# Setting a chunk's weights with a predicated copy, and moving half of the diagonal into the skip factor

## The chip, the cores and the metric

The kernel runs on one core of one Trainium2 chip. The metric is the time of one execution in microseconds (us) of device time. Five engines work side by side, each through its own queue in order: TensorE (PE, with its weight loads shown as PEld), VectorE (DVE), ScalarE (ACT), GpSimd (POOL) and SyncE (SP), which issues most DMAs.

## What is computed

Two layers of a bidirectional encoder trunk on a sequence of 2048 tokens with 1024 channels. The change lies in the second layer, in the Mamba-2 heads (8 heads of 64 channels in 2 groups, state size 128). Cut to what matters:

```python
def dir_inputs(dt_raw, d):
    dt = softplus(dt_raw + dt_bias[d])
    return xs * dt[..., None], dt * (-exp(a_log[d]))

x_fw, a_fw = dir_inputs(dt_f, 0)
x_bw, a_bw = dir_inputs(dt_b, 1)
y = (ssd_chunked(x_fw, a_fw, bm, cm)
     + rev(ssd_chunked(rev(x_bw), rev(a_bw), rev(bm), rev(cm)))
     + d_skip[:, None] * xs)
y = rms_norm(y.reshape(bsz, seq, WIDTH_D) * silu(dz), ssm_norm_g)
return concat([yc, y], -1) @ w_out        # then the residual and a layer norm
```

Inside a chunk, `ssd_chunked` multiplies three things for a query token i and a key token j: the product of C at i and B at j, the decay between the two tokens, and the input at j, which carries the factor dt of that direction. The forward direction holds for j up to and including i, the backward direction for j from i on. On the diagonal, j = i, both directions count and the decay is one.

## The kernel before, in words

The sequence is cut into 16 chunks of 128 tokens. The first layer and the input projections of the second run first; the last stage of the program, from about 2315 us on, is a loop over the chunks c = 0 to 15 that ends each chunk's Mamba-2 output, and behind it the output projection of the whole layer.

For a chunk, `Ssd.local` loads tokens (`tk`), B and C (`bc`), the gate (`dzl`) and the backward state (`sbl`). On PE it makes `pcb`, the products of B and C of both groups, 128 x 256 in one bank of PSUM. For each group g of four heads it makes the decay exponents in the bank `pd`: POOL (L1246) and ACT (L1249) fill `rr`, four matmuls sum it (L1250, L1251), and ACT writes the exponential into `E` (L1253). The weights `w`, 128 x 512 for a group, take dt of the forward direction where j <= i and dt of the backward one where j >= i: per head, ACT multiplies the triangle `le` by the forward dt (L1256), and DVE multiplies the triangle `ge` by the backward dt and adds (L1257). Then DVE multiplies `E` by `pcb` (L1259) and `w` by `E` (L1260).

`Ssd.forward` uses the weights one chunk later: the matmuls `py` (L1273), the skip term (POOL, L1276: tokens times `dskip`, a factor per head), the sum (L1277), the contributions of the two states (`pin` on PE L1281, `ti` on DVE L1285, added on POOL L1286), the state's update (`pu` L1211, `sf` L1219 and L1220), the gate (L1292), the norm (L1294 to L1297), a transpose into the bank `pt` (L1300) and `syo` (DVE, L1302). `OutProj.steps` is the output projection with the layer norm: it splits `syo` and the other heads' `yr` into a high and a low part (ACT L1003, DVE L1004), runs 48 matmuls a chunk into `oo` (L1032), and DVE, ACT and POOL do the rest (L1039 to L1050).

Three things tie the engines here. `E` has one buffer, the tag `cvt`. The bank `pd` is single too. `pcb` and `pt` share one bank, so the `pcb` of chunk c+1 can be made only when `syo` of the chunk before has read `pt`. The order on each engine is set by a scheduler at build time; the four queues are then fixed. In three of the chunks a pass over the other kind of heads (`pass_b`, with `pob`, `stw`, `opl`) is put between, up to about 2547 us.

Of the kernel before, what the change touches and what calls it, by code (L numbers as in the profile page):

```python
# [10 lines left out]
F32 = mybir.dt.float32  # L11
F32R = mybir.dt.float32r
I32 = mybir.dt.int32
AF = mybir.ActivationFunctionType
ALU = mybir.AluOpType
AX = mybir.AxisListType
# [3 lines left out]
P = 128  # L20
# [410 lines left out]
class Rec:  # L431
# [14 lines left out]
    def bank(self, name):  # L446
        return self.ps.tile([P, 512], F32, name=name, tag="rg", bufs=self.e.rg_bufs)
# [616 lines left out]
class Ssd:  # L1064
# [157 lines left out]
    def local(self, c, pool, bank):  # L1222

        e, nc = self.e, self.e.nc
        cs = slice(c * P, (c + 1) * P)
        k = self.cur[c] = Env()
        kp = self.kp
        k.tk = kp.tile([P, 768], F32, name="tk", tag="tk", bufs=2)
        nc.sync.dma_start(k.tk, self.tok[cs, :])
        k.bc = kp.tile([P, 4, P], F32, name="bc", tag="cvx", bufs=2)  # L1230
        nc.sync.dma_start(k.bc, self.xc[:, :, cs])
        k.dz = kp.tile([P, 512], F32, name="dzl", tag="sb", bufs=2)
        nc.sync.dma_start(k.dz, self.dz[cs, :])
        k.sb = kp.tile([P, 512], F32, name="sbl", tag="cva", bufs=2)
        nc.sync.dma_start(k.sb, self.sbd[c])
        pcb = bank("pcb")
        for g in range(2):
            nc.tensor.matmul(pcb[:, g * P:(g + 1) * P], k.bc[:, g], k.bc[:, 2 + g], start=True, stop=True)
        k.w = pool.tile([P, 2, 4, P], F32, name="w", tag="Q", bufs=2)
        for g in range(2):  # L1240
            pd = bank("pd")
            w = k.w[:, g]
            for d, (m1, m2) in enumerate((("gt", "le"), ("lt", "ge"))):
                r = pool.tile([P, 2, 4, P], F32R, name="rr", tag=f"T{d}", bufs=1)
                h0 = d * 8 + g * 4
                nc.gpsimd.tensor_tensor(r[:, 0], e.tri[m2].unsqueeze(1).broadcast_to([P, 4, P]),  # L1246
                                        self.aH[:, c, h0:h0 + 4].unsqueeze(2).broadcast_to([P, 4, P]), ALU.mult)
                for h in range(4):
                    nc.scalar.activation(r[:, 1, h], e.tri[m2], AF.Copy, scale=self.aL[:, c, h0 + h:h0 + h + 1])  # L1249
                nc.tensor.matmul(pd, e.trir[m1], r[:, 0], start=d == 0, stop=False)  # L1250
                nc.tensor.matmul(pd, e.trir[m1], r[:, 1], start=False, stop=d == 1)  # L1251
            E = kp.tile([P, 4, P], F32, name="E", tag="cvt", bufs=1)
            nc.scalar.activation(E, pd.rearrange("p (h i) -> p h i", h=4), AF.Exp)  # L1253
            for h in range(4):
                hh = g * 4 + h
                nc.scalar.activation(w[:, h], e.tri["le"], AF.Copy, scale=self.dt[:, c, hh:hh + 1])  # L1256
                nc.vector.scalar_tensor_tensor(w[:, h], e.tri["ge"], self.dt[:, c, 8 + hh:9 + hh], w[:, h],  # L1257
                                               ALU.mult, ALU.add)
            nc.vector.tensor_tensor(E, E, pcb[:, g * P:(g + 1) * P].unsqueeze(1).broadcast_to([P, 4, P]), ALU.mult)  # L1259
            nc.vector.tensor_tensor(w, w, E, ALU.mult)  # L1260

    def forward(self, c, pool, bank):
        e, nc = self.e, self.e.nc
        cs = slice(c * P, (c + 1) * P)
        h8 = lambda t: t.rearrange("p (h q) -> p h q", h=8)
        k = self.cur.pop(c)
        tk, bc, dz, sb = k.tk, k.bc, k.dz, k.sb
        if c == 0:
            self.sf = pool.tile([P, 512], F32, name="sf", tag="qm0", bufs=1)
            nc.gpsimd.memset(self.sf, 0.0)  # L1270
        py = bank("py")
        for hh in range(8):
            nc.tensor.matmul(py[:, hh * 64:(hh + 1) * 64], k.w[:, hh // 4, hh % 4], tk[:, hh * 64:(hh + 1) * 64],  # L1273
                             start=True, stop=True)
        acc = pool.tile([P, 512], F32, name="yacc", tag=f"{'kq'[c % 2]}m1", bufs=1)
        nc.gpsimd.tensor_tensor(h8(acc), h8(tk[:, :512]), self.dskip.unsqueeze(2).broadcast_to([P, 8, 64]), ALU.mult)  # L1276
        nc.vector.tensor_tensor(acc, py, acc, ALU.add)  # L1277
        for d, st in ((0, self.sf), (1, sb)):
            po = bank("pin")
            for g in range(2):  # L1280
                nc.tensor.matmul(po[:, g * 256:(g + 1) * 256], bc[:, 2 + g], st[:, g * 256:(g + 1) * 256],  # L1281
                                 start=True, stop=True)
            t = pool.tile([P, 512], F32, name="ti", tag=f"Sf{d}", bufs=1)
            eq = self.ed["qf" if d == 0 else "qb"][:, c, :].unsqueeze(2).broadcast_to([P, 8, 64])
            nc.vector.tensor_tensor(h8(t), h8(po), eq, ALU.mult)  # L1285
            nc.gpsimd.tensor_tensor(acc, acc, t, ALU.add)  # L1286
        if c < NC - 1:
            pu = self.update(self.weighted(c, 0, tk, pool), tk[:, 512:], bank)
            new = pool.tile([P, 512], F32, name="sf", tag=f"{'kq'[c % 2]}m0", bufs=1)
            self.step(new, self.sf, c, 0, pu)  # L1290
            self.sf = new
        nc.vector.tensor_tensor(acc, acc, dz, ALU.mult)  # L1292
        ss = pool.tile([P, 1], F32, name="sss", tag="ss", bufs=4)
        nc.scalar.activation(t, acc, AF.Square, accum_out=ss)  # L1294
        nc.gpsimd.tensor_scalar(ss, ss, 1.0 / 512, 1e-6, ALU.mult, ALU.add)
        nc.gpsimd.tensor_tensor(ss, ss, e.mhalf[:, 0:1], ALU.pow)
        nc.scalar.activation(acc, acc, AF.Copy, scale=ss)  # L1297
        pt = bank("pt")
        for i in range(4):
            nc.tensor.transpose(pt[:, i * P:(i + 1) * P], acc[:, i * P:(i + 1) * P], e.ident)  # L1300
        yo = pool.tile([P, 4, P], F32, name="syo", tag="kd", bufs=1)
        nc.vector.tensor_tensor(yo, pt.rearrange("p (a b) -> p a b", a=4),  # L1302
                                self.gcol.unsqueeze(2).broadcast_to([P, 4, P]), ALU.mult)
        return yo
# [50 lines left out]
def trunk(ctx, tc, i, out):  # L1355
    nc = tc.nc
    e = Env()
# [5 lines left out]
    def const(name, shape, dt=F32):  # L1363
        t = cp.tile(list(shape), dt, name=f"c_{name}")
        nc.sync.dma_start(t, i[name])
        return t
# [9 lines left out]
    def opened(name, side, **kw):  # L1376
        cm = tc.tile_pool(name=name, bufs=1, reuse_waits="tile", side=side, **kw)
        pools[name] = cm
        return cm.__enter__()
# [169 lines left out]
    hg = const("hgrn_g", [P, 1])  # L1549
    sg_ = const("ssm_g", [P, 4])  # L1550
    e.tri = {m: const(f"t_{m}", [P, P]) for m in TRI}
    e.trir = {}
    for m in ("gt", "lt"):
        e.trir[m] = cp.tile([P, P], F32R, name=f"r_{m}")
# [24 lines left out]
    kp = opened("conv", "left")  # L1579
# [104 lines left out]
def layout(inp):  # L1684

    f = lambda n: np.ascontiguousarray(inp[n])
    r = {}
# [28 lines left out]
    t, j = a[:, None], a[None, :]  # L1716
    for nm, m in (("gt", t > j), ("lt", t < j), ("le", t <= j), ("ge", t >= j)):
        r["t_" + nm] = m.astype(np.float32)
    lm = np.zeros((P, 5, 32), np.int32)
    i32 = np.arange(32)  # L1720
    for l in range(5):
# [21 lines left out]
```

## Time and profile before

| | us |
|---|---|
| median of 3 runs | 2748.59 |
| lowest and highest | 2747.47 to 2750.7 |
| the profiled execution, its own time | 2755.94 |
| its span from the first instruction to the last | 2754.1 |
| the last stage, from 2315 us on | 439 |

The profiled execution is one run with the profiler on; its rows show when each instruction started on its engine and how long it took. Over the whole span PE is busy 92%, DVE 54%, ACT 41% and POOL 48%; in the last stage DVE is busy six to nine tenths of each slice but the final one. An instruction's shown duration overlaps with the next one's by 0.06 to 0.09 us on DVE, so that an instruction shown with 0.68 us holds the queue for about 0.60.

### The profile page before, as it was taken

To read this page: it belongs to the slowest core of one execution; us is meant where nothing else is said; L and a number is where in the kernel's file an instruction comes from. 1 tells how busy PE (TensorE), PEld (TensorE's weight loads), DVE (VectorE), ACT (ScalarE), POOL (GpSimd) and SP (SyncE) were. 2 spreads that over 40 slices of the span, in tenths; PEclk is the share of its full clock that TensorE was granted. 3 is DMA by queue.
4 is the path that set the end of the run, shared out by engine and by line. 5 is a ranking of instruction groups with operands and counts; after the bars stand their busy time and mean duration, and the time that the engine had idled before them with its cause. 6 is when DMAs were issued, how large, how long until landed. Compare 5 with 4: busy or idle time off the path is not lost. (4 is left out here: it accounts for less than half of the span.)

```text
span 2754.1 us, 53110 instructions
## 1 busy us (share of the span) xinstructions
PE 2526.8 (92%) x20888; PEld 2125.2 (77%) x20888; DVE 1493.4 (54%) x2493; ACT 1122.9 (41%) x2355; POOL 1326.1 (48%) x1305
## 2 busy tenths in 40 slices
PE   7999999999999799998999999999999888788987
PEld 5877778887778677877788777888877677566776
DVE  6223335124433676765626356432625788687895
ACT  3152323244343644543323444232424453554652
POOL 4252325244442544434535556335534677575874
PEclk9999999999999899999999999999999999798998
DMA  8525434323365878775553335434436567543331
GB/s 275 159 99 169 145 115 132 115 95 106 109 221 181 253 210 234 202 205 167 173 201 126 106 124 177 136 127 131 134 105 207 169 200 235 182 148 112 117 115 62
DMA packets 269800, 432.46 MB, mean 157 GB/s; under 512 B 25936, under 2 KB 143600, under 8 KB 269552
## 3 DMA queue, kind: packets, MB, share of 16 engines
q1 hardware_dynamic: 267248, 420.69, 48.7%
q0 software_dynamic: 2304, 8.39, 0.8%
q8 instruction: 165, 2.70, 0.4%
q14 instruction: 83, 0.68, 0.1%
HBM read 296.60 MB, written 132.38 MB: 156 GB/s over the span
## 5 line engine op out<-in xcount | busy, mean ns | idle before, releaser
L186 POOL TENSOR_TENSOR wl<-wraw,wh 128x1024 fp32r<-128x1024 f32 (+2 forms) x116 | 290.5, 2524 | 293.9 <-ACT wh L185 293.0
L1032 PE MATMUL oo<-wo,yH 128*128 128x512 f32 x1024 | 309.9, 418 | 21.8 <-ACT yH L1003 20.2
L536 POOL TENSOR_TENSOR Kp<-Kp,T 128x256 f32<-128x256 f32 x144 | 125.7, 873 | 275.1 <-ACT F L492 111.7
L1032 PEld LDWEIGHTS oo<-wo,yH 128*128 128x128 f32 x1024 | 199.8, 201 | 65.3 <-ACT yH L1003 23.5
L860 POOL TENSOR_TENSOR nap<-nap,nasm 128x384 f32<-128x384 f32 (+2 forms) x128 | 115.7, 914 | 209.5 <-DVE nasm L859 192.2
L534 DVE TENSOR_TENSOR Kp<-Kp,T 128x256 f32<-128x256 f32 x144 | 103.7, 720 | 146.6 <-PE fine L459 60.2
L185 ACT CAST wh<-wraw 128x1024 fp32r<-128x1024 f32 (+2 forms) x116 | 116.8, 1052 | 154.5 <-PE obqk L205 27.4
L1032 PE MATMUL oo<-wo,yL 128*128 128x512 f32 x512 | 172.4, 405 | 3.0 <-DVE yL L1004 3.0
L532 DVE TENSOR_TENSOR Q<-Q,T 128x512 f32<-128x512 f32 x144 | 146.9, 1020 | 0.0
L885 PE MATMUL nay<-napts,nav 128*128 128x128 f32 (+1 forms) x832 | 121.5, 289 | 20.2 <-ACT napts L872 13.7
L885 PEld LDWEIGHTS nay<-napts,nav 128*128 128x128 f32 (+1 forms) x832 | 114.5, 202 | 31.3 <-ACT napts L872 16.1
L1154 DVE SCALAR_TENSOR_TENSOR cva<-cvx,cw,cva 128x512 f32<-128x512 f32 x96 | 104.2, 1098 | 30.5 <-ACT cva L1152 29.4
L1032 PEld LDWEIGHTS oo<-wo,yL 128*128 128x128 f32 x512 | 97.5, 193 | 23.5 <-DVE yL L1004 4.2
L205 PE MATMUL oqf<-hH,wh 128*128 128x512 f32 x256 | 104.8, 409 | 4.5 <-ACT wh L185 4.5
L205 PE MATMUL ox<-hH,wh 128*128 128x512 f32 x256 | 106.2, 415 | 0.0
L497 DVE COPY_PREDICATED S<-lmask,fine 128x128 f32<-128x128 int32 x160 | 43.7, 297 | 111.3 <-PE fine L459 111.2
L205 PE MATMUL ox<-hH,wl 128*128 128x512 f32 x256 | 102.7, 401 | 0.0
L205 PE MATMUL ox<-hL,wh 128*128 128x512 f32 x256 | 102.5, 400 | 0.0
L205 PE MATMUL oqf<-hL,wh 128*128 128x512 f32 x256 | 102.4, 400 | 0.0
L205 PE MATMUL oqf<-hH,wl 128*128 128x512 f32 x256 | 101.9, 399 | 0.5 <-POOL wl L186 0.5
L858 ACT ACTIVATE nap<-nap,namx 128x384 f32<-128x384 f32 (+2 forms) x128 | 79.2, 619 | 50.6 <-DVE namx L857 50.3
L156 POOL TENSOR_TENSOR hL<-hf,hH 128x512 fp32r<-128x512 f32 x36 | 50.2, 1403 | 96.9 <-ACT hH L155 96.9
(375 smaller groups left out, 7723.8 us busy)
## 6 DMA issues: line engine op xcount, KB each, us to landing
wraw<-in_o_w_dram SPq DMA_DIRECT2D x56, 512.0 KB
wraw<-in_e_w_dram SPq DMA_DIRECT2D x44, 512.0 KB
adw<-in_ada_w_dram SPq DMA_DIRECT2D x32, 512.0 KB
tk<-xtok SPq DMA_DIRECT2D x31, 384.0 KB
nat<-in_na_tab_dram SPq DMA_DIRECT2D x16, 640.0 KB
xt<-in_x_dram SPq DMA_DIRECT2D x16, 512.0 KB
adw<-in_ada_p_dram SPq DMA_DIRECT2D x16, 512.0 KB
naq<-aq SPq DMA_DIRECT2D x64, 128.0 KB
```

Of the source, the lines that this page charges most:

```text
L156: (nc.vector if d % 2 and not act else nc.gpsimd).tensor_sub(hL[:, d, :], hf, hH[:, d, :].bitcast(F32))
L185: nc.scalar.copy(h[:, sl], raw)
L186: (nc.vector if e.wl_dve else nc.gpsimd).tensor_sub(l[:, sl], raw, h[:, sl].bitcast(F32))
L205: nc.tensor.matmul(oo, a, b, start=d == 0 and m == 0, stop=d == ND - 1 and m == 2)
L532: nc.vector.tensor_tensor(qv, qv, view(tcur, toff + 1, [[nb - 1, 2], [2, n2], [0, s]]), ALU.mult)
L534: nc.vector.tensor_tensor(kv, kv, view(tcur, toff + nb + 1, [[2, n2], [0, s]]), ALU.mult)
L536: nc.gpsimd.tensor_tensor(kv, kv, view(tcur, toff, [[2, n2], [0, s]]), ALU.mult)
L858: nc.scalar.activation(p[:, :nk], p[:, :nk], AF.Exp, bias=mx, scale=-1.0, accum_out=sm)
L860: nc.gpsimd.tensor_tensor(p[:, :nk], p[:, :nk], sm.broadcast_to([P, nk]), ALU.mult)
L885: nc.tensor.matmul(s.yp[:, n, :], b.vs[:kb, n, j, :], s.pts[n][:kb, j, :], start=j == 0, stop=j == nj - 1)
L1032: nc.tensor.matmul(os[n], ops[m][0][:, c, :], ops[m][1][c][:, ns], start=x == 0, stop=x == 23)
L1154: nc.vector.scalar_tensor_tensor(acc, xr[:, k:k + SW], cw[:, i, k:k + 1], acc, ALU.mult, ALU.add)
```

## The change

The weights of a group are set by two instructions instead of eight. ACT writes the backward dt, spread over the columns, into all 512 columns (`nc.scalar.copy`), and DVE overwrites the places where j <= i with the forward dt by a predicated copy under an integer mask, `lei`, which is a new constant of 128 x 128 that SP loads once. The diagonal then holds the forward dt alone. Its backward share, dt of the backward direction times the product of B and C at the token itself, is added to the skip factor instead: DVE takes the diagonal of `pcb` (multiply by the identity into `own`, then a sum along the row into `cd`), multiplies it by the backward dt and adds `dskip`; the result `skip` is the factor in POOL's skip term. `own` lies in the same single buffer `cvt` as `E`.

```diff
         pcb = bank("pcb")
...
+        own = kp.tile([P, 2, P], F32, name="own", tag="cvt", bufs=1)
+        nc.vector.tensor_tensor(own, pcb[:, :2 * P].rearrange("p (g i) -> p g i", g=2),
+                                e.ident.unsqueeze(1).broadcast_to([P, 2, P]), ALU.mult)
+        cd = pool.tile([P, 2], F32, name="cd", tag="cd", bufs=2)
+        nc.vector.tensor_reduce(cd, own, AX.X, ALU.add)
+        k.skip = pool.tile([P, 2, 4], F32, name="skip", tag="skip", bufs=2)
+        nc.vector.tensor_tensor(k.skip, self.dt[:, c, 8:].rearrange("p (g h) -> p g h", g=2),
+                                cd.unsqueeze(2).broadcast_to([P, 2, 4]), ALU.mult)
+        nc.vector.tensor_tensor(k.skip, k.skip, self.dskip.rearrange("p (g h) -> p g h", g=2), ALU.add)
...
-            for h in range(4):
-                hh = g * 4 + h
-                nc.scalar.activation(w[:, h], e.tri["le"], AF.Copy, scale=self.dt[:, c, hh:hh + 1])
-                nc.vector.scalar_tensor_tensor(w[:, h], e.tri["ge"], self.dt[:, c, 8 + hh:9 + hh], w[:, h],
-                                               ALU.mult, ALU.add)
+            dts = [self.dt[:, c, d * 8 + g * 4:d * 8 + g * 4 + 4].unsqueeze(2).broadcast_to([P, 4, P]) for d in range(2)]
+            nc.scalar.copy(w, dts[1])
+            nc.vector.copy_predicated(w, e.lei.unsqueeze(1).broadcast_to([P, 4, P]), dts[0])
...
-        nc.gpsimd.tensor_tensor(h8(acc), h8(tk[:, :512]), self.dskip.unsqueeze(2).broadcast_to([P, 8, 64]), ALU.mult)
+        nc.gpsimd.tensor_tensor(h8(acc), h8(tk[:, :512]), k.skip.rearrange("p g h -> p (g h)").unsqueeze(2).broadcast_to([P, 8, 64]), ALU.mult)
...
+    e.lei = const("t_lei", [P, P], I32)
```

The scheduler orders the queues anew from about 2315 us on; what stands ahead of that is as before, save for the mask's load. On DVE, one chunk in the middle of the loop stood like this before (`syo` and `yL` belong to the chunk that is ending, `w` and `E` to the chunk that is prepared):

```order
L1302 TENSOR_TENSOR syo<-pt,c_ssm_g 128x512
L1277 TENSOR_TENSOR yacc<-py,yacc 128x512
L1285 TENSOR_TENSOR ti<-pin,edqf 128x512
L1285 TENSOR_TENSOR ti<-pin,edqb 128x512
L1004 TENSOR_TENSOR yL<-syo,yH 128x512
L1257 SCALAR_TENSOR_TENSOR w<-c_t_ge,dt,w 128x128
L1259 TENSOR_TENSOR E<-E,pcb 128x512
L1257 SCALAR_TENSOR_TENSOR w<-c_t_ge,dt,w 128x128 x4
L1220 TENSOR_TENSOR sf<-sf,pu 128x512
L1257 SCALAR_TENSOR_TENSOR w<-c_t_ge,dt,w 128x128 x2
L1260 TENSOR_TENSOR w<-w,E 128x512
L1257 SCALAR_TENSOR_TENSOR w<-c_t_ge,dt,w 128x128
```

On DVE after the change, the same place of a chunk near the end of the loop (`own` and `cd` are the diagonal, L1266 is the predicated copy):

```order
L1285 TENSOR_TENSOR yacc<-py,yacc 128x512
L1004 TENSOR_TENSOR yL<-syo,yH 128x512
L1266 COPY_PREDICATED w<-c_t_lei,dt 128x512
L1241 TENSOR_TENSOR own<-pcb,c_ident 128x256
L1266 COPY_PREDICATED w<-c_t_lei,dt 128x512
L1293 TENSOR_TENSOR ti<-pin,edqf 128x512
L1244 TENSOR_REDUCE cd<-own 128x2
L1300 TENSOR_TENSOR yacc<-yacc,dzl 128x512
L1246 TENSOR_TENSOR skip<-dt,cd 128x8
L1039 SCALAR_TENSOR_TENSOR r<-r,oo 128x512
L1248 TENSOR_TENSOR skip<-skip,dskip 128x8
```

What moved: the eight multiply-adds went, the two predicated copies stand in their place, and the first reader of `pcb` is now `own`, at once behind the first copy, where it had been the multiply of `E`.

On PE, around a transpose `pt` and the next `pcb`, after the change (L1260 and L1261 are now the `pd` matmuls, L1281 `py`, L1289 `pin`):

```order
L1260 MATMUL pd<-rr,r_gt 128x512
L1261 MATMUL pd<-rr,r_gt 128x512
L1308 MATMUL pt<-c_ident,yacc 128x128 x4
L1260 MATMUL pd<-rr,r_lt 128x512
L1261 MATMUL pd<-rr,r_lt 128x512
L1281 MATMUL py<-tk,w 128x64 x4
L1289 MATMUL pin<-sf,bc 128x256 x2
L1289 MATMUL pin<-sbl,bc 128x256 x2
L1238 MATMUL pcb<-bc 128x128 x2
L1032 MATMUL oo<-wo_23903,yH 128x512
```

And before, in one of the chunks where the same pieces stood together:

```order
L1250 MATMUL pd<-rr,r_lt 128x512
L1300 MATMUL pt<-c_ident,yacc 128x128 x4
L1251 MATMUL pd<-rr,r_lt 128x512
L1273 MATMUL py<-tk,w 128x64 x4
L1281 MATMUL pin<-sf,bc 128x256 x2
L1281 MATMUL pin<-sbl,bc 128x256 x2
L1238 MATMUL pcb<-bc 128x128 x2
L1250 MATMUL pd<-rr,r_gt 128x512
L1251 MATMUL pd<-rr,r_gt 128x512
L1211 MATMUL pu<-xw,tk 128x256 x2
```

What moved: behind `pcb` now stand the projection's matmuls, where the next `pd` had followed; `pcb` still stands behind `py` and both `pin`.

## Rows read from the trace of the kernel before

**Rows 1.** Busy time by stretch; the first line names the columns.
```profile
core 0: us, PE busy (x) PEld busy (x) DVE busy (x) ACT busy (x) POOL busy (x), PEclk, DMA share, GB/s
...
2402.00:2547.00 145.00, 121.78 (x568) 100.24 (x567) 115.42 (x168) 67.43 (x190) 92.09 (x93) 0.91 0.40 129
2547.00:2700.00 153.00, 138.74 (x672) 114.51 (x671) 137.74 (x196) 88.83 (x255) 112.19 (x113) 0.96 0.36 115
2700.00:2754.00 54.00, 41.48 (x183) 33.22 (x181) 26.88 (x42) 11.82 (x20) 20.81 (x22) 0.90 0.13 49
```

**Rows 2.** The chain that ended last, shares by line, 2547 to 2700 us.
```profile
by line: PE oo L1032 28.5%; DVE w L1257 25.3%; issue 4.7%; DVE r L1048 3.6%; PE pin L1281 3.6%; PE py L1273 3.4%; DVE w L1260 3.1%; DVE yL L1004 2.7%; DVE yacc L1292 2.5%; ACT rr L1249 2.2%; DVE E L1259 2.1%; DVE ti L1285 1.7%; DVE sf L1220
```

**Rows 3.** DVE's groups, 2402 to 2700 us: busy, mean ns | idle before, releasers.
```profile
L1257 DVE SCALAR_TENSOR_TENSOR w<-c_t_ge,dt,w 128x128 f32<-128x128 f32 x96 | 75.3, 835 | 2.3 <-ACT w L1256 2.3
...
L1260 DVE TENSOR_TENSOR w<-w,E 128x512 f32<-128x512 f32 x26 | 24.7, 951 | 0.3
...
L1259 DVE TENSOR_TENSOR E<-E,pcb 128x512 f32<-128x512 f32 x26 | 17.6, 677 | 7.5 <-ACT E L1253 3.8 <-PE pcb L1238 3.6
```

**Rows 4.** DVE in order of time in one chunk: start, us, instruction.
```profile
2616.93 0.67 DVE L1259 TENSOR_TENSOR E<-E,pcb 128x512 f32<-128x512 f32 x1
2617.53 4.17 DVE L1257 SCALAR_TENSOR_TENSOR w<-c_t_ge,dt,w 128x128 f32<-128x128 f32 x4
```

**Rows 5.** POOL in the same microseconds.
```profile
2618.12 1.09 POOL L1246 TENSOR_TENSOR rr<-c_t_le,aH 128x512 fp32r<-128x512 f32 x1
2619.17 1.33 POOL L1286 TENSOR_TENSOR yacc<-yacc,ti 128x512 f32<-128x512 f32 x1
2620.47 1.09 POOL L1203 TENSOR_TENSOR xw<-tk,edkf 128x512 f32<-128x512 f32 x1
```

**Rows 6.** Single lines over the whole span: ns min/median/max, first and last start, forms.
```profile
L1257 DVE SCALAR_TENSOR_TENSOR w<-c_t_ge,dt,w x128: 292/527/1446, 2318.8 to 2687.2; 128x128 f32<-128x128 f32 x128
L1260 DVE TENSOR_TENSOR w<-w,E x32: 672/692/1777, 2354.0 to 2713.8; 128x512 f32<-128x512 f32 x32
L497 DVE COPY_PREDICATED S<-lmask,fine x160: 274/297/309, 168.1 to 2323.8; 128x128 f32<-128x128 int32 x160
L396 DVE TENSOR_TENSOR st<-st,odz x32: 401/410/422, 1764.9 to 2334.6; 128x256 f32<-128x256 f32 x32
L1042 DVE BATCH_NORM_AGGREGATE mv<-bst x32: 180/200/210, 1004.6 to 2746.5; 128x2 f32<-128x12 f32 x32
L1256 ACT ACTIVATE w<-c_t_le,dt x128: 384/388/403, 2317.8 to 2679.0; 128x128 f32<-128x128 f32 x128
L1003 ACT CAST yH<-syo x16: 602/618/622, 2402.7 to 2734.1; 128x512 fp32r<-128x512 f32 x16
```

**Rows 7.** The chain's PE pieces, 2600 to 2650 us: start, us, what.
```profile
2610.64 0.24 PE pd L1250
...
2611.35 0.44 PE pt L1300 x4
...
2612.02 0.84 PE py L1273 x8
2612.85 1.80 PE pin L1281 x8
...
2635.81 0.44 PE pcb L1238 x4
2636.25 5.49 PE oo L1032 x24
...
2642.14 0.92 PE pu L1211 x4
```

**Rows 8.** Waits, 2402 to 2700 us: us in total, times, longest.
```profile
ACT E L1253 <- DVE w L1260: 17.4, 7, 6.9
...
PE pcb L1238 <- DVE syo L1302: 5.7, 3, 4.1
...
PE pd L1250 <- ACT E L1253: 4.3, 1, 4.3
```

More of the change, by code (lines that the diff above doesn't have):

```diff
@@ L1718, in layout @@
         r["t_" + nm] = m.astype(np.float32)
+    r["t_lei"] = (t <= j).astype(np.int32)
     lm = np.zeros((P, 5, 32), np.int32)
```

## The prediction, made before the changed kernel ran

> **What bounds the kernel now.** Read the busy time by stretch first, then the chain that ended last, then DVE's groups, and last two engines side by side. The change touches only the loop over chunks, so the stretches from 2402 us on are the ones to read; 12 of the 16 chunks have their weights made between 2402 and 2700 us (96 multiply-adds, 8 a chunk [rows 3]). In that stretch DVE is busy 115.4 of 145 us and then 137.7 of 153 us [rows 1]: 253 of 298. PE looks as busy, but its ends are modelled. What it needs is read from the chain's pieces [rows 7]: a chunk has two runs of 24 `oo` (2 x 5.49), 8 `pd` of 0.24, `pt` 0.44, 16 `py` (2 x 0.84), `pin` 1.80, `pcb` 0.44 and `pu` 0.92, together 18.2 us, against the 298 / 12 = 24.8 us that a chunk takes in the stretch as a whole. So PE has room, and DVE has little.
>
> The chain says the same. In 2547 to 2700 us the multiply-adds of L1257 hold 25.3% of it, second only to the projection [rows 2]: 0.253 x 153 = 38.7 us, 5.5 us for each of the 7 chunks there.
>
> Why they are so dear: one takes 292 ns at best, but 835 ns in the mean of the stretch [rows 3, 6]. Four of them in a row took 4.17 us [rows 4], one for each POOL instruction that ran in the same microseconds, each of 1.1 to 1.3 us [rows 5]. Which instructions suffer can be told apart. `E` times `pcb`, with one input in PSUM, takes 677 ns in the mean; `w` times `E`, of the same size with both inputs in SBUF, takes 951 [rows 3]. The predicated copy that the kernel has elsewhere, with its data in PSUM, never took over 309 ns in 160 times [rows 6]. So an instruction of DVE with two inputs in SBUF waits until POOL's present one is over, and eight small ones wait eight times.
>
> **The change part by part.** *Removed on DVE:* 96 multiply-adds, 75.3 us of DVE's time in the stretch [rows 3], 6.3 us a chunk.
>
> *Added on DVE, predicated copies:* 24, of 512 columns. The trace has this operation only with 128 columns and data in PSUM, 297 ns [rows 6]. Here mask and data both lie in SBUF. The lower bound is the instruction of that size that never waits, 677 ns, the upper one the longest that `w` times `E` took, 1777 ns [rows 3, 6]. I take the mean of `w` times `E`, by its kind of inputs the nearest row: 24.7 / 26 = 0.95, so 24 x 0.95 = 22.8 us.
>
> *Added on DVE, the diagonal:* `own` is 256 columns with one input in PSUM, as the row of L396: 410 ns [rows 6], less about 0.07 of overlap 0.34. The sum along the row reads 256 columns from one tile; no such operation is in the trace, and I take the same 0.34, between 0.20 (the aggregate on 12 numbers) and 0.68 (512 columns) [rows 3, 6]. Both: 12 x 0.68 = 8.2 us.
>
> *Added on DVE, the skip factor:* two instructions of 8 columns with two inputs in SBUF. Without a wait they cost what the aggregate costs, 0.20 less 0.07; with the full wait of the worst multiply-add (1446 - 292 ns) [rows 6] 1.15 us more. I add the mean wait of `w` times `E`, 951 - 677 = 0.27, and round to 0.35 with what the short overlap loses: 24 x 0.35 = 8.4 us, between 3 and 31.
>
> DVE's sum: 75.3 - 22.8 - 8.2 - 8.4 = 35.9 us less in the stretch, 3.0 a chunk. With the low ends it is 75.3 - 16.2 - 6.5 - 3 = 50; with the high ends 75.3 - 42.6 - 12.2 - 31 = -10, a loss.
>
> *How much of this shows.* In 2547 to 2700 us most of the removed time is on the chain (38.7 us, where 7 of 12 chunks hold 43.9 of the 75.3 us of multiply-adds), so the net share of it, 35.9 / 75.3 = 0.48, is gained: 38.7 x 0.48 = 18.5 us. From 2402 to 2547 us no chain is to be had; DVE stands idle 30 of 145 us there, and PE too waits more [rows 1]. The other 31.4 us of multiply-adds lie there, net 15; I count half, 7 us, since only some of DVE's queue can be what PE waits for in a stretch where both wait. Before 2402 and after 2700 us nothing is counted: in the tail no weights are made any more, and the first stretch waits for the last projections. Sum: 25.5 us.
>
> *ACT:* per chunk eight of 388 ns go and two writes of 512 columns come, 618 ns by the cast of that size [rows 6]: 1.9 us less. ACT is busy 88.8 of 153 us [rows 1] and holds little of the chain [rows 2], so this counts as nothing; what hides it is DVE's queue, and if that got so short that ACT was next, it would be a gain of at most 1.9 us a chunk. *POOL:* the same number of instructions; its skip term now waits for `skip`, which is made a chunk earlier, so nothing. *PE:* no instruction added. *SP:* one load of 64 KB with the other constants, over a millisecond ahead of its first use.
>
> *New waits.* `own` stands in DVE's queue behind one predicated copy, before `ti`, the gate and the layer norm's instructions, and needs `pcb`. On PE `pcb` stands behind `pt`, two `pd`, half of the `py`, and `pin`, which end 0.48 + 0.84 + 1.80 + 0.44 = 3.6 us after `pt`. In that time DVE does `syo`, `yacc` and `yL` at about 0.6 each and a copy at 0.95, 2.8 us, and `yL` waits for ACT's cast of 0.62 in between [rows 6]. The wait left is some 0.2 us, near the noise of the sum. Second, `E` can be filled only when the sum along the row has read `own`. So far it waited for `w` times `E` of the group before, 17.4 us in 7 times [rows 8]. The sum stands three to five instructions ahead of the reader of `E`, which covers ACT's exponential (about the 0.62 of the cast) or most of it. I cost both at nothing, and put the case that they aren't under the rivals.
>
> **A rule of the skill against the row.** The rows above show that 512 columns with both inputs in SBUF cost 951 ns and with one in PSUM 677. The Trainium skill, SBUF — State Buffer, section Who interferes with whom, says that a Vector instruction with two SBUF inputs contends with a GpSimd instruction that reads SBUF, that whichever starts first holds the shared port for its whole length, and that a reduction along the row does not contend. By that rule the predicated copies stay exposed to POOL and the result is as above; if a predicated copy did not contend, 24 x 0.27 = 6.5 us more of DVE's time would go and the gain would be about 30 us. No row shows a predicated copy with two SBUF inputs.
>
> **The rivals.** *1. More: PE sets the pace.* If DVE's relief counts whole in both stretches, the 298 us fall by all of the 36 us, and by 50 with the low ends. For it speaks the 18.2 us that PE needs in 24.8; against it, the shares of the chain in which DVE, PE and ACT alternate. Time, with the middle of the two, 43: 2748.6 - 43 = 2706.
>
> *2. Absorbed.* PE, POOL and ACT wait for each other as well: POOL is busy 112.2 of 153 us [rows 1], and its instructions have the other side of every wait with DVE. If the chain goes over to POOL and PE as soon as DVE is shorter, or the new order loses in its first chunks what the later ones gain, the gain is 0 to 5 us. Against it speaks that 25% of the chain is one line. Time: 2746.
>
> *3. Slower: `own` blocks DVE's queue.* If `pcb` is late, `own` holds everything behind it, the layer norm of the chunk included, and the sum behind it delays `E`, the `pd` of the second group and so PE. The price is the wait per chunk; it decides from 3.0 us on, where it eats all that DVE saves. Waits of such lengths occur: `pcb` waited up to 4.1 us for `syo`, `pd` 4.3 for `E` [rows 8]. With 4.1 in each of 12 chunks it is 12 x (4.1 - 3.0) = 13 us slower, 2762. Against it: `pcb` was late in 3 of the chunks alone.
>
> **How the numbers follow.** The profiled execution took 2755.9 us, 7.3 more than the median of the runs, 2748.6; I take the same 25.5 us from both: 2730.4 with the profiler, 2723 without. Chances: the forecast (10 to 38 us less) 0.64; rival 1 0.08; rival 2 0.17; rival 3 with the high ends of the new instructions 0.11. About 0.2% (5.5 us) is what a measurement of this kernel can tell from no change. Rival 2 lies within that line and counts as the same, with 0.01 of the case with the high ends: faster 0.64 + 0.08 = 0.72, same 0.18, slower 0.10. The range runs from 2703, which takes in most of rival 1, to 2747, about the middle of rival 2; some 0.15 is left out above and 0.04 below.
>
> **What would show it.** Right: L1257 is gone, the copies of L1266 take 0.9 to 1.0 us in the mean with a least value near 0.68, `own` near 0.41 always; DVE is busy about 215 us in the 12 chunks' stretch, which is 20 to 30 us shorter; the tail from the last `w` times `E` on is as long as before, 40 us (2713.8 to 2754 [rows 6]); the waits `own` <- `pcb` and `E` <- sum are a few us in all. Wrong: copies at 1.5 us or more, the two small instructions over 0.8 us each, a wait for `pcb` or for ACT's `E` of several us in each chunk, or a chain in which POOL has taken DVE's share.

## The result and the profile after

| | before | after |
|---|---|---|
| median, us | 2749.64 | 2715.24 |
| ratio after to before, 95% interval | | 0.9872, 0.9845 to 0.9898 |
| the same two kernels again, in other runs, us | 2751.30 | 2720.31 |
| ratio of these, 95% interval | | 0.9879, 0.9863 to 0.9895 |
| the profiled execution's span, us | 2754.1 | 2709.5 |

The kernel became 1.2 to 1.3% faster by the two ratios, 31 to 34 us by the medians, against 25.5 us in the forecast of 2723. The stretch ahead of the loop has the same instructions in all kernels here, save for the mask's load, but ends between 2300 and 2319 us from one profiled execution to another; why, no run here shows. Totals of single executions so differ by up to 19 us before the loop begins. The comparisons below therefore use the **loop time** of a profiled execution as well: from the last start of `cva`, an instruction of the first layer, to the end of the span. The rows of that mark, the kernel before and the one after (ns min/median/max, first and last start):

```profile
L1154 DVE SCALAR_TENSOR_TENSOR cva<-cvx,cw,cva x96: 735/752/2897, 1609.7 to 2312.3; 128x512 f32<-128x512 f32 x96
```
```profile
L1154 DVE SCALAR_TENSOR_TENSOR cva<-cvx,cw,cva x96: 736/752/2899, 1602.3 to 2304.3; 128x512 f32<-128x512 f32 x96
```

The loop takes 2754.1 - 2312.3 = 441.8 us before and 2709.5 - 2304.3 = 405.2 after, 36.6 less. A second profiled execution of the changed kernel gave 407.0. Cut at the same events (the layer norm's `mv` of chunks 0, 5 and 13), the loop has four pieces; the rows are cut to whole microseconds. Before:

```profile
core 0: us, PE busy (x) PEld busy (x) DVE busy (x) ACT busy (x) POOL busy (x), PEclk, DMA share, GB/s
2312.00:2412.00 100.00, 76.07 (x513) 63.95 (x512) 69.61 (x125) 51.97 (x159) 54.63 (x58) 0.80 0.58 197
2412.00:2547.00 135.00, 112.13 (x518) 92.25 (x518) 106.45 (x155) 64.50 (x184) 88.00 (x89) 0.90 0.40 130
2547.00:2714.00 167.00, 152.74 (x741) 126.29 (x740) 145.49 (x209) 92.00 (x260) 117.26 (x118) 0.96 0.35 112
2714.00:2754.00 40.00, 27.48 (x114) 21.43 (x112) 19.13 (x29) 8.64 (x15) 15.74 (x17) 0.87 0.10 40
```

After:

```profile
2304.00:2399.00 95.00, 73.57 (x515) 61.62 (x515) 66.35 (x112) 46.28 (x132) 53.42 (x56) 0.82 0.60 205
2399.00:2514.00 115.00, 106.89 (x514) 88.58 (x513) 93.56 (x147) 57.67 (x154) 90.76 (x88) 0.96 0.48 154
2514.00:2676.00 162.00, 151.52 (x753) 124.48 (x752) 130.44 (x201) 84.89 (x222) 128.75 (x122) 0.99 0.36 116
2676.00:2709.00 33.00, 23.11 (x108) 18.48 (x106) 17.02 (x29) 7.20 (x12) 13.69 (x14) 0.95 0.12 48
```

Read the lengths first. By the events themselves 99.9, 135.2, 166.3 and 40.4 us became 94.6, 115.0, 162.7 and 33.0; the second execution of the changed kernel has 95.4, 114.3, 164.1 and 33.2, so that one or two microseconds of a piece say nothing. The largest part of the gain, 20 us, is in the second stretch, where the passes over the other heads lie between the chunks; 5 us are in the first, 4 in the third, and 7 in the tail, where no weights are made. Then read DVE: 106.45 + 145.49 = 251.9 us in the two middle stretches before, 93.56 + 130.44 = 224.0 after, 27.9 less, while POOL in the third rose from 117.26 of 167 to 128.75 of 162.

DVE's lines after, from 2399 to 2676 us (busy, mean ns of one | idle before them), which answer to [rows 3]:

```profile
L1266 DVE COPY_PREDICATED w<-c_t_lei,dt 128x512 f32<-128x512 int32 x24 | 24.8, 1051 | 3.0 <-ACT w L1265 3.0
L1048 DVE SCALAR_TENSOR_TENSOR r<-r,mv,lng 128x512 f32<-128x512 f32 x26 | 21.6, 869 | 0.1
L1268 DVE TENSOR_TENSOR w<-w,E 128x512 f32<-128x512 f32 x26 | 19.3, 743 | 0.2
...
L1246 DVE TENSOR_TENSOR skip<-dt,cd 128x8 f32<-128x8 f32 x13 | 7.8, 597 | 0.0
L1241 DVE TENSOR_TENSOR own<-pcb,c_ident 128x256 f32<-128x256 f32 x13 | 5.3, 412 | 0.0
L1244 DVE TENSOR_REDUCE cd<-own 128x2 f32<-128x256 f32 x13 | 5.3, 411 | 0.2
L1248 DVE TENSOR_TENSOR skip<-skip,dskip 128x8 f32<-128x8 f32 x13 | 3.4, 258 | 0.0
```

The same lines over the whole span (ns min/median/max), beside [rows 6]:

```profile
L1266 DVE COPY_PREDICATED w<-c_t_lei,dt x32: 706/728/1840, 2310.8 to 2650.6; 128x512 f32<-128x512 int32 x32
L1241 DVE TENSOR_TENSOR own<-pcb,c_ident x16: 407/413/425, 2326.5 to 2668.7; 128x256 f32<-128x256 f32 x16
L1244 DVE TENSOR_REDUCE cd<-own x16: 396/420/421, 2327.1 to 2669.2; 128x2 f32<-128x256 f32 x16
L1246 DVE TENSOR_TENSOR skip<-dt,cd x16: 150/168/1254, 2328.6 to 2670.1; 128x8 f32<-128x8 f32 x16
```

The spread between least and most tells which of them wait for POOL: the copy and the small product, each with two inputs in SBUF, take up to 1.1 us more than their best; `own`, with one input in PSUM, and the sum along the row never take more than 25 ns over theirs. That is as the Trainium skill, SBUF — State Buffer, section Who interferes with whom, has it: two SBUF inputs contend with GpSimd, a reduction does not; the section names no predicated copy, and here the copy contends. Read one by one in the trace, the 13 of the 32 copies that took over 0.95 us all ended 0.58 to 0.60 us after an instruction of POOL had ended.

The chain of waits in the third stretch after, which answers to [rows 2]:

```profile
by line: PE oo L1032 18.8%; POOL rr L1256 8.6%; POOL yacc L1294 6.6%; issue 6.6%; POOL r L1050 6.2%; DVE yL L1004 5.1%; DVE w L1266 4.4%; DVE r L1039 3.8%; PE pin L1289 2.7%; POOL sf L1219 2.5%; DVE bst L1040 2.4%; POOL rs L1045 2.3%; DVE y
```

Where the multiply-adds held 25.3%, the copies hold 4.4%, and POOL's lines, none of which stands in that row of before, hold 26.2% with the five that are shown here.

### The profile page after: what moved, and what is told of

Same layout as the page of the kernel before. It is cut to its first block, busy times and chain, and to the rows that moved or that the text cites. A ratio compares the mean times of both kernels' runs of the same rounds, so it can differ in the third digit from the quotient of the medians.

```text
span 2709.5 us, 52970 instructions
## 1 busy us (share of the span) xinstructions
PE 2501.7 (92%) x20888; PEld 2106.1 (78%) x20888; DVE 1457.4 (54%) x2461; ACT 1101.3 (41%) x2259; POOL 1340.4 (49%) x1305
## 4 chain that ended last, share of the span: by engine, by line
PE 33%; DVE 8%; DMA 7%; POOL 5%; issue 3%; ACT 3%; SPq 2%; POOLq 0%; DVEq 0%; ACTq 0%
PE oqf L205 7%; PE oo L1032 6%; PE ox L205 3%; PE ob L205 3%; PE og L205 2%; PE oci L205 2%; PE odz L205 2%; DVE cva L1154 2%; DMA nak<-ak 1%; DMA cvx<-xbc 1%; PE fine L459 1%; SPq L810 1%; DMA Kp<-cz 1%; PE nay L885 1%; POOL rr L1256 1%
## 5 line engine op out<-in xcount | busy, mean ns | idle before, releaser
L1032 PE MATMUL oo<-wo,yH 128*128 128x512 f32 x1024 | 300.7, 407 | 18.2 <-ACT yH L1003 17.2
L1032 PEld LDWEIGHTS oo<-wo,yH 128*128 128x128 f32 x1024 | 192.7, 194 | 59.3 <-ACT yH L1003 21.5
L185 ACT CAST wh<-wraw 128x1024 fp32r<-128x1024 f32 (+2 forms) x116 | 116.7, 1051 | 153.5 <-PE obqk L205 25.8
L1032 PEld LDWEIGHTS oo<-wo,yL 128*128 128x128 f32 x512 | 95.9, 190 | 25.3 <-DVE yL L1004 6.7
```

Source lines behind the costliest of these rows:

```text
L185: nc.scalar.copy(h[:, sl], raw)
L1032: nc.tensor.matmul(os[n], ops[m][0][:, c, :], ops[m][1][c][:, ns], start=x == 0, stop=x == 23)
```

## The experiments

All loop times are from one profiled execution each, and the one kernel that was profiled twice differs by 1.8 us; medians and ratios are from the timed runs, against the kernel before on the same chip. DVE's busy time holds its waits for POOL too, since an instruction that has started and waits counts as busy. Two theories stood against each other. **A**: DVE's work sets the loop's time, and the change gains because it takes work off DVE. **B**: the gain comes from the order and the new tie (`own` in the buffer of `E`), which the scheduler made of the change, and DVE's work matters little. One table for all, with the busy time of DVE and POOL in the loop:

| kernel | median, us | ratio (95%) | loop, us | DVE | POOL |
|---|---|---|---|---|---|
| before | | | 441.8 | 340.4 | 275.3 |
| after | 2715.24 | 0.9872 (0.9845 to 0.9898) | 405.2 | 307.1 | 286.3 |
| after, again | 2720.31 | 0.9879 (0.9863 to 0.9895) | 407.0 | 308.9 | 287.9 |
| e1 copy alone | 2724.74 | 0.9887 (0.9858 to 0.9917) | 409.1 | 307.4 | 288.4 |
| e2 diagonal alone | 2736.57 | 0.9940 (0.9917 to 0.9962) | 429.3 | 328.7 | 282.7 |
| e3 copy twice | 2737.76 | 0.9939 (0.9918 to 0.9959) | 427.6 | 328.2 | 286.5 |
| e4 before, spaced | 2755.10 | 1.0010 (0.9996 to 1.0025) | 445.4 | 339.3 | 276.9 |
| e5 own buffer | 2724.89 | 0.9903 (0.9877 to 0.9930) | 411.2 | 311.7 | 283.8 |
| e6 before, tied | 2730.68 | 0.9931 (0.9909 to 0.9953) | 426.3 | 326.8 | 279.0 |
| e7 eight writes | 2717.45 | 0.9880 (0.9849 to 0.9912) | 403.1 | 314.8 | 288.4 |
| e8 POOL relieved | 2705.29 | 0.9834 (0.9807 to 0.9861) | 398.4 | 313.6 | 268.2 |
| e9 own buffer, ordered | 2720.54 | 0.9897 (0.9878 to 0.9916) | 412.4 | 314.2 | 289.5 |
| e10 e9 and e8 | 2714.97 | 0.9871 (0.9854 to 0.9887) | 398.1 | 309.6 | 270.7 |
| e11 POOL relieved twice | 2724.74 | 0.9897 (0.9881 to 0.9913) | 410.6 | 302.0 | 246.4 |

**One part alone: e1 and e2.** e1 is the changed kernel without the diagonal's part (it leaves out the backward share on the diagonal):

```diff
-        own = kp.tile(...)
...
-        nc.gpsimd.tensor_tensor(..., k.skip ..., ALU.mult)
+        nc.gpsimd.tensor_tensor(..., self.dskip ..., ALU.mult)
```

> The changed kernel without the diagonal's part: own, cd and the two skip instructions go, the skip factor is dskip again (the backward share on the diagonal is left out). Theory A, DVE's work decides: some 16 us less of DVE's time than the changed kernel in the 12 chunks, so 2698 to 2710 us. Theory B, the scheduler's order decides: without own the scheduler again puts the state matmuls pin of three chunks in a row on PE in the middle of the loop, as before, with no projection between, so most of the gain of the chunks with the pass between is lost: 2722 to 2740 us, although DVE has less to do.

e2 has the diagonal's part, and the eight multiply-adds of before under the mask `gt`:

```diff
...
-            nc.scalar.copy(w, dts[1])
-            nc.vector.copy_predicated(w, ..., dts[0])
+            for h in range(4):
...
+                nc.scalar.activation(w[:, h], e.tri["le"], AF.Copy, scale=...)
+                nc.vector.scalar_tensor_tensor(w[:, h], e.tri["gt"], ..., w[:, h], ALU.mult, ALU.add)
```

> The kernel before with the diagonal's part alone: eight activations and eight multiply-adds a group pair stay (with the strict triangle gt), own, cd and skip are added. Theory A, DVE's work decides: 12 x 1.4 us more on DVE, so slower than before by 10 to 17 us, 2760 to 2767. Theory B, the order decides: own ties the chunks so that the state matmuls stand in regular places as in the changed kernel; 15 to 25 us gained by that, up to 17 lost on DVE: 2735 to 2750, not slower than before.

The copy alone brings 32.7 of the 36.6 us of loop time. The medians of e1 and e2 lie in the ranges that B gave, not in those of A. Yet B had most of the gain lost in e1, and e1's ratio is not told apart from that of the whole change; and A had DVE less busy in e1 than after, and it is not (307.4 us for 307.1). So neither theory holds as it was put. The surprise is e2: it adds 64 instructions to DVE, takes none away, and its loop is 12.5 us shorter, the median 14.6 us. DVE is not busier for it but 11.7 us less busy. The multiply-adds, over the loop, of before, of e2 and of e6 below:

```profile
L1257 DVE SCALAR_TENSOR_TENSOR w<-c_t_ge,dt,w 128x128 f32<-128x128 f32 x128 | 89.7, 750 | 2.4 <-ACT w L1256 2.4
```
```profile
L1267 DVE SCALAR_TENSOR_TENSOR w<-c_t_gt,dt,w 128x128 f32<-128x128 f32 x128 | 63.8, 546 | 3.2 <-ACT w L1266 3.2
```
```profile
L1261 DVE SCALAR_TENSOR_TENSOR w<-c_t_ge,dt,w 128x128 f32<-128x128 f32 x128 | 65.3, 566 | 4.8 <-ACT w L1260 4.7
```

The same 128 instructions wait less: 89.7 us became 63.8. Read one by one, 67 of them took over 0.41 us before, 33 in e2 and 34 in e6, and every one of these ended 0.14 to 0.16 us after an instruction of POOL had ended: what fell is the number of waits for POOL. In e1, without the diagonal, the copies wait more than after, 1296 ns in the mean against 1010:

```profile
L1257 DVE COPY_PREDICATED w<-c_t_lei,dt 128x512 f32<-128x512 int32 x32 | 40.1, 1296 | 3.9 <-ACT w L1256 3.9
```
```profile
L1266 DVE COPY_PREDICATED w<-c_t_lei,dt 128x512 f32<-128x512 int32 x32 | 31.8, 1010 | 3.0 <-ACT w L1265 3.0
```

So the diagonal's part pays for itself on DVE: its instructions cost DVE about 26 us in the loop (32 of 0.41 and 16 each of 0.516 and 0.292 in the mean, by the groups of the whole loop), and e1 and after are equally busy.

**DVE's work added back: e3.** The predicated copy is issued twice; the second changes nothing in `w`:

```diff
             nc.vector.copy_predicated(w, e.lei..., dts[0])
+            nc.vector.copy_predicated(w, e.lei..., dts[0])
```

> The changed kernel with each predicated copy issued twice: 24 more in the 12 chunks, about 1.0 us each. If DVE still sets the pace: 20 to 28 us slower than the changed kernel, 2735 to 2743. If POOL and PE set it now and DVE has room: 0 to 12 us slower, 2715 to 2727.

The loop became 22.4 us longer (20.6 against the second execution), while DVE's busy time rose by 21.1. In the third stretch, 162 us after, it is 177:

```profile
2531.00:2708.00 177.00, 163.18 (x760) 130.38 (x759) 138.29 (x218) 84.89 (x222) 125.89 (x122) 0.95 0.33 106
```

DVE is 7.9 us busier there, and the stretch grew by 14 between the events; PE's busy time grew too, by 11.7 for seven matmuls more, at a granted clock of 0.95 for 0.99. So work put back on DVE shows whole, as theory A has it.

**The order alone: e4.** The kernel before, where the second half of a chunk (`forward`) may be placed only behind the projection of two chunks before, so that no three chunks' `pin` and `pu` run in a row:

```diff
+        with tc.issue_after(op.ends[c - 2]) if c > 1 else ExitStack():
+            yo = sd.forward(c, mp, sbank)
...
```

> The kernel before with one rule for the order: what a chunk's forward part issues on PE stands behind the last projection matmul of two chunks earlier, so that no three chunks stand together. No instruction is added or removed. Theory A, DVE's work decides: within 5 us of before, 2745 to 2755. Theory B, the order decides: 10 to 20 us faster than before, 2730 to 2740.

The two middle stretches:

```profile
2406.00:2532.00 126.00, 105.54 (x505) 87.10 (x504) 105.71 (x153) 65.25 (x187) 87.34 (x89) 0.91 0.41 134
2532.00:2720.00 188.00, 160.84 (x765) 132.17 (x764) 146.81 (x215) 93.01 (x261) 121.98 (x121) 0.93 0.32 103
```

The first fell from 135 to 126 us, the second rose from 167 to 188 (with some of the tail's work, since chunk 13 ends later); DVE's time is as before, and so is the total. A more even order of this kind gains nothing, which speaks against B in that form.

**The tie: e5 and e6.** e5 gives `own` a buffer of its own, so that `E` no longer waits for the sum along the row:

```diff
-        own = kp.tile([P, 2, P], F32, name="own", tag="cvt", bufs=1)
+        own = self.wp.tile([P, 2, P], F32, name="own", tag="own", bufs=1)
...
```

> The changed kernel with a buffer of its own for own, so that E no longer waits until the row sum has read own. No instruction is added or removed. In the build's order the state matmuls pin of three chunks stand together on PE again, as before the change. Theory B, the shared buffer ties each chunk's weights to the chunk before and so makes the order regular: 5 to 15 us slower than the changed kernel, 2720 to 2730. Theory A, the shared buffer is only a wait (ACT waited 22.5 us for it between 2402 and 2660 us): 0 to 10 us faster, 2705 to 2715.

e6 is the kernel before with the tie and nothing else: two copies of 8 columns go through the buffer of `E` behind `pcb`:

```diff
+        tie = kp.tile([P, 2, P], F32, name="tie", tag="cvt", bufs=1)
+        nc.vector.tensor_copy(tie[:, 0, :8], pcb[:, P:P + 8])
...
+        nc.vector.tensor_copy(k.tied, tie[:, 0, :8])
```

> The kernel before with the tie alone: a copy of 8 columns of pcb into a tile in E's buffer and a copy out of it, two small instructions on DVE (some 0.3 us a chunk, 4 us in all); the weights are made as before. Theory B, the tie's order is worth 15 to 30 us: 2720 to 2735, faster than the run with the whole diagonal added (2736.6), which has 13 us more on DVE. Theory A, DVE's work alone counts: 2750 to 2756.

Taking the wait away did not help: e5's loop is 6.0 us longer, and its ratio is higher by 0.0024 to 0.0031 with intervals that overlap, so the ratio does not tell the two apart. In its place POOL waits for `skip`, which the scheduler now makes late: e5 and, behind it, after.

```profile
POOL yacc L1284 <- DVE skip L1248: 13.8, 6, 3.5
```
```profile
POOL yacc L1284 <- DVE skip L1248: 3.3, 4, 1.4
```

Adding the tie to the kernel before, in e6, made its loop 15.5 us shorter, 0.69% by the ratio, though DVE got 32 instructions more. DVE's busy time fell by 13.6 us; the multiply-adds alone fell from 89.7 to 65.3 (the third of the rows above), with half as many waits for POOL. So B has a share, and the medians of e5 and e6 lie in its ranges: under the tie the scheduler makes another order, in which DVE's small instructions meet fewer of POOL's. That DVE is busy for 327 to 329 us in e2, e3 and e6 alike, and their loops take 426 to 429, looks as if the order acted through DVE's time alone, as A would have it. The four pieces, by the events, say otherwise:

| kernel | first, us | second | third | tail |
|---|---|---|---|---|
| before | 99.9 | 135.2 | 166.3 | 40.4 |
| after | 94.6 | 115.0 | 162.7 | 33.0 |
| e1 copy alone | 97.6 | 118.3 | 158.5 | 34.7 |
| e2 diagonal alone | 97.1 | 125.0 | 174.3 | 32.9 |
| e3 copy twice | 99.4 | 118.9 | 176.4 | 33.0 |
| e6 before, tied | 99.4 | 123.2 | 170.7 | 33.1 |

Of e6's 15.5 us, 7.3 are in the tail, where no multiply-adds are; e2 has 7.5 of its 12.5 there. In the second stretch both gain 10 to 12 us, and in the third both lose, 4 and 8 us. So the order acts partly through DVE's waits and partly through how much of the projection is left for the end, and the like totals of the three kernels are made up of unlike pieces.

**The tie's place in the order: e9 and e10.** e9 is e5 with the scheduler told to keep the exponential into `E` behind the sum along the row, in order alone and without a wait:

```diff
-            nc.scalar.activation(E, pd..., AF.Exp)
+            ex = nc.scalar.activation(E, pd..., AF.Exp)
+            if g == 0:
+                e.tc.add_manual_dep(ex.ins, behind.ins.name, ... NoSync ...)
```

> The changed kernel with own in a buffer of its own (as in e5_own_buffer), and the order alone kept: the exponential of a chunk's first group is placed behind the row sum in the build, with no wait for it on the chip. The PE queue is regular again, no three chunks' pin together. If the order is what the shared buffer brings: as the changed kernel or a little faster, 2705 to 2718, and 7 to 15 us under e5_own_buffer. If the wait itself paces the engines to advantage: as e5_own_buffer, 2720 to 2730.

The wait for `skip` is down to 5.7 us, but the loop, 412.4 us, stayed where e5 was (411.2), so that place in the order is not what makes e5's loop longer. As neither ratio is told apart from that of the changed kernel, it is not shown that the tie helps there at all. e10 is e9 with the edit of e8 (below):

> e9_own_order and e8_pool_relief together. If the wait for E still costs something where POOL no longer sets the pace: 2695 to 2704. If POOL's relief was all there is to gain: 2703 to 2710.

Its loop, 398.1 us, is that of e8 with the tie (398.4), while its ratio is higher, 0.9871 for 0.9834, with intervals that overlap: the tie is no loss there either. Its median lies above both of its ranges. Beside e9, which differs from it by the edit of e8 alone, its loop is 14.3 us shorter and its median 5.6, by intervals that just overlap.

**ACT's relief: e7.** The backward dt is written by eight instructions of 128 columns, as many as ACT had before:

```diff
-            nc.scalar.copy(w, dts[1])
+            for h in range(4):
+                nc.scalar.activation(w[:, h], e.ones, AF.Copy, scale=...)
```

> The changed kernel with ACT's two wide writes replaced by eight of 128 columns, as many as before the change: some 1.9 us a chunk more on ACT, nothing else. If ACT's relief counts for nothing, as the prediction held: within 6 us of the changed kernel, 2709 to 2721. If it was part of the gain: 8 to 20 us slower, 2723 to 2735.

ACT is busy 20 us more in the loop, 216.1 against 196.0, and the loop, 403.1 us, is no longer than after; nor is the ratio told apart. ACT's relief is worth nothing that these runs show, as forecast. (DVE too is 7.7 us busier in it; so the loop's time does not follow DVE's to the microsecond.)

**What is late next: e8 and e11.** Of POOL's four products `rr` a chunk, e8 makes one on ACT, in four instructions of 128 columns; e11 makes two there (the condition is `d == 1` alone). e8's edit:

```diff
-                nc.gpsimd.tensor_tensor(r[:, 0], e.tri[m2]..., self.aH..., ALU.mult)
+                if g == 1 and d == 1:
+                    for h in range(4):
+                        nc.scalar.activation(r[:, 0, h], e.tri[m2], AF.Copy, scale=...)
+                else:
+                    nc.gpsimd.tensor_tensor(r[:, 0], e.tri[m2]..., self.aH..., ALU.mult)
```

> The changed kernel with one of POOL's four products rr of a chunk made by ACT in four pieces instead: 1.1 to 1.2 us less on POOL a chunk, 1.6 more on ACT. If POOL, busy 129 of 160 us between 2500 and 2660 us and the largest part of the chain beside PE, sets the pace now: 8 to 15 us faster, 2700 to 2707. If it does not: within 5 us of 2715, or slower if ACT's queue then holds E.

> The changed kernel with two of POOL's four products rr of a chunk made by ACT (2.2 us less on POOL, 3.2 more on ACT a chunk). If POOL still sets the pace after the first: another 5 to 10 us, 2695 to 2701. If ACT, DVE or PE is next: 2703 to 2715.

The third stretch of e8, its row and its chain:

```profile
2517.00:2671.00 154.00, 149.10 (x754) 124.20 (x753) 132.74 (x201) 94.93 (x255) 117.38 (x114) 1.00 0.38 121
```
```profile
by line: PE oo L1032 28.8%; issue 7.1%; DVE w L1270 6.8%; DVE yL L1004 5.1%; PE pin L1293 4.2%; PE py L1285 3.8%; DVE r L1039 3.2%; ACT rr L1263 2.8%; DVE yacc L1304 2.6%; PE pd L1264 2.3%; PE pd L1265 2.3%; DVE ti L1297 2.1%; DVE E L1271 2
```

162 us became 154 with POOL 11.4 us less busy, though DVE was 2.3 us busier. POOL has left the head of the chain. The gain ends there: the third stretch of e11 has

```profile
2530.00:2690.00 160.00, 151.90 (x751) 126.47 (x750) 126.47 (x203) 104.75 (x289) 105.76 (x105) 0.98 0.36 116
```

POOL and DVE are both less busy than in e8, and it is 6 us longer, with ACT's `rr` first behind PE in its chain (6.4% and 3.8%, by its two lines). The median of e11, 2724.74, lies above both ranges that were given for it. e8 has the lowest ratio that ran: 0.9834, an interval of 0.9807 to 0.9861, against 0.9872 and 0.9879 for the change alone. Its interval overlaps the first of these, and e10, with the same edit, has 0.9871; by the loop times, from one execution each, both gain: 7 us against after, and 14 against e9.

**The change once more.**

> The changed kernel once more, on the chip of the other three, to compare them with: 2711 to 2720.

It repeats: 407.0 us of loop against 405.2, and the ratios of the two sets overlap nearly whole.

## Why the prediction was right, and where its sum was not

**DVE's time counts: shown. That DVE alone sets the pace is not.** e3 puts 21.1 us back on DVE and the loop takes 22.4 longer; e1 takes 33.0 off it and the loop takes 32.7 less. Once the multiply-adds are gone, the loop no longer follows DVE alone: beside the changed kernel e8 has DVE busy for 6.5 us more and its loop is 6.8 us shorter, e11 has 5.1 less and is 5.4 longer. The forecast put DVE at some 215 us in the stretch of the 12 chunks, and that stretch 20 to 30 us shorter: it is 224.0 us, in a stretch of 277 for 302.

**The removed and added work: 28.7 us instead of 35.9.** Removed was 75.3 as taken. The 24 copies took 24.8 us for 22.8 (1051 ns for 950; over the whole loop 1010, with a least value of 706 for the 0.68 expected). `own` and the sum took 10.6 in 13 chunks for 8.2 in 12, 0.41 each as the row of L396 said, without the overlap that I took off. The skip factor's two took 11.2 for 8.4: 597 ns for the first, 258 for the second, 0.43 in the mean for 0.35. So 75.3 - 24.8 - 10.6 - 11.2 = 28.7; other lines gained and lost about as much (`w` times `E` 24.4 us to 19.3, `yL` 20.2 to 28.6), and 27.9 remain.

**How much of it shows: the step that failed.** I let 0.48 of the chain's share count in the stretch from 2547 us on, 18.5 us, and half of 15 in the one ahead, 7. Measured were 4 and 20, in sum 24 for 25.5, and that the sum agrees is luck. It is most of DVE's 27.9 us, as rival 1 had it, and it lies at other places than I put it. The other 13 us of the gain lie in the first stretch and the tail, which were counted at zero.

In the second stretch the term was "I count half, 7 us, since only some of DVE's queue can be what PE waits for". PE's waits in that stretch, before:

```profile
PE pin L1281 <- DVE sf L1220: 6.9, 3, 3.1
PE pd L1250 <- ACT E L1253: 4.3, 1, 4.3
PE pcb L1238 <- DVE syo L1302: 4.1, 1, 4.1
PE pu L1211 <- POOL sss L1296: 2.8, 1, 2.8
PE pt L1300 <- ACT yacc L1297: 2.8, 1, 2.8
PE py L1273 <- DVE w L1260: 1.2, 1, 1.2
PE pd L1250 <- POOL rr L1246: 0.7, 1, 0.7
```

and after, all of them:

```profile
PE pin L1289 <- DVE sf L1220: 3.9, 1, 3.9
PE py L1281 <- issue: 1.9, 1, 1.9
PE oo L1032 <- DVE yL L1004: 1.2, 2, 1.0
PE oo L1032 <- ACT yH L1003: 0.7, 1, 0.7
PE pcb L1238 <- DVE syo L1310: 0.3, 1, 0.3
PE pu L1211 <- DVE ti L1293: 0.2, 1, 0.2
```

22.8 us of waits became 8.2: 14.6 of the 20. Another 5.2 us is PE's own busy time, 112.13 to 106.89 for about as many matmuls (518 and 514), at a granted clock of 0.96 for 0.90: waiting less, PE also ran faster. Of the 22.8 us, 12.2 were on DVE itself, but those on ACT and POOL went as well. Halving left both out, the second link behind a wait and the clock. How much of these 20 us is DVE's shorter work and how much the new order is not told apart here: e1 has 118 us in this stretch, e2 125 and e6 123, for 135 before and 115 after. The forecast had no term for a gain by the order: it stood there as something that could lose (rival 2), and its tie as a wait, costed at nothing. Put into the kernel before by itself, in e6, that tie was worth 15.5 us.

In the third stretch the chain's share was no price. DVE had 15.1 us less to do there and 4 were gained, and POOL's lines moved up to 26.2% of the chain. That is rival 2 at that one place, and the sign that the prediction gave for being wrong, a chain in which POOL has taken DVE's share. e8 shows it by taking POOL's share away, and e10 beside e9 once more: that stretch becomes 8 and 12 us shorter. The skip term on POOL, costed at nothing, waited 3.3 us for `skip` in the whole loop, too little to be the reason.

**The tail and the first stretch, counted at zero: 7 and 5 us.** From the last `w` times `E` to the end it was 40.3 us before, and 2709.5 - 2676.6 = 32.9 after; the prediction had named an unchanged tail as a sign of being right. The last pieces of PE in the chain, before and after:

```profile
2722.36 0.67 PE pt L1300 x4
...
2724.45 8.28 PE oo L1032 x24
...
2734.69 10.30 PE oo L1032 x44
```
```profile
2688.79 0.66 PE pt L1308 x4
2689.45 11.06 PE oo L1032 x48
```

Before, 68 matmuls of the projection were left behind the last transposes, after only 48: the projection of chunk 14 was done earlier. At 11.06 / 48 = 0.23 us each the 20 make 4.6 us. The other 2.8 us are in the first 24 of before, which took 8.28 us for 5.5 at that rate: the mean granted clock was 0.69 there (2722 to 2733 us), and 1.00 after (2689 to 2700 us). e6 ends in 33.0 us too, with all multiply-adds kept, so this piece is the order's and not the removed work's; e1 has 34.0, so it does not need the tie. The first stretch's 5 us I can't assign.

**The waits.** `own` waited 1.2 us for `pcb`, once in 16 chunks: rival 3 fell. The other new wait was larger than costed, here from 2399 to 2676 us:

```profile
ACT E L1263 <- DVE cd L1244: 26.3, 7, 4.6
```

It takes the place of 17.4 us in [rows 8]. That it costs the loop anything is not to be seen: e5, without it, is not faster.

**What stays open.** How the 36.6 us divide between the shorter work and the new order: e1 alone has 32.7 and e6 alone 15.5, together more than the whole, and no run takes the work away with the order held. Why the tie in e6 makes DVE wait less for POOL: a more even order (e4) did not do so, and the order without the wait (e9) ran only in the changed kernel; that the wait itself moves DVE's small instructions out of POOL's way would fit, but no run shows it. Nor is the tie needed for most of the gain, as e1 has none.

## What to carry to other kernels

Price instructions that share a port by what they wait, and count how often they can wait: one instruction of 512 columns can wait once where four of 128 can wait four times. Before the chain's share of a line is taken for the price of removing it, look at which engine is next; here the net relief of DVE over the whole loop came nearer to the gain than the share in any one stretch. Where a scheduler sets the order, measure each part alone, for the order itself can gain: here 15.5 us by a tie alone, in the kernel before. When the first engine is relieved, try to move a product off the next one; here one product helped, and a second lost the gain again.

## What the runs showed of the hardware

A predicated copy of 512 f32 columns with mask and data in SBUF took 706 ns at best, 728 in the median and up to 1840 beside POOL; with data in PSUM the 128-column one never went beyond 309 [rows 6]. An instruction of 8 columns with two SBUF inputs, 150 ns at best, took up to 1254. A sum along the row over 256 columns took 396 to 421 ns in all 16 instances. A multiply-add of 128 columns with two SBUF inputs took 292 ns at best, and each of the 67 that took over 0.41 us in the loop before ended 0.14 to 0.16 us after an instruction of POOL.
